# The first norm's sum of squares: eight products with ones on TensorE in place of seven adds on VectorE

## The chip, the cores and the metric

The kernel runs on one core of one Trainium2 chip. The metric is the device time of one execution in microseconds (us); a kernel's time is the median of its runs.

## The reference

One inference step of a two-layer decoder trunk over 576 tokens: 512 of a prompt and 8 sequences of 8 new tokens. The model is 1024 wide; everything is fp32.

```python
def rmsnorm(x, w):
    xf = x.astype(jnp.float32)
    y = xf * lax.rsqrt(jnp.mean(xf * xf, axis=-1, keepdims=True) + EPS)
    return (y * w.astype(jnp.float32)).astype(x.dtype)
...
def layer(x, ...):
    h = rmsnorm(x, P['norm_mix_w'][li])
    proj = jnp.einsum('bld,de->ble', h, P['w_in'][li]).astype(jnp.float32)
    (z, xbc, dt_raw, q_a, k_a, v_a, q_h, f_h, i_h, g_h, x_r, g_r) = jnp.split(proj, SPLIT_POINTS, axis=-1)
    # four mixers on the parts of proj: SSD (Mamba-2), sliding-window attention, HGRN2, RG-LRU
...
    mix = jnp.concatenate([y_ssd, y_swa, y_hg, y_lru], axis=-1).astype(dtype)
    x = x + jnp.einsum('ble,ed->bld', mix, P['w_out'][li])
    h2 = rmsnorm(x, P['norm_mlp_w'][li])
    up = jnp.einsum('bld,df->blf', h2, P['w_up'][li])
    x = x + jnp.einsum('blf,fd->bld', jnp.square(jax.nn.relu(up)), P['w_down'][li])
```

The norm that the change touches is the first `rmsnorm` of layer 0.

## The kernel before

x is held transposed: eight blocks `self.x[k]` of 128 features by 576 tokens. A product on TensorE has 128 features as its contraction and 288 tokens, half of them, as its columns; a weight matrix comes in tiles of 128 output columns with all 1024 features (`raw`, 512 KB each, loaded by SyncE's queue). To keep fp32 accuracy at the speed of the one-pass type fp32r, weights and activations are split into a high and a low part: `weight` (L326) makes `hi` on ScalarE and `lo` on VectorE, `norm` (L377, L378) makes `xh` on ScalarE and `xl` on VectorE, and each tile takes three products per feature block and half (`product`, L339): xh·hi, xl·hi, xh·lo, 24 to a half. The products of the projection are called `pi` in the profile.

The norm's weight is folded into `xh` and `xl`; the factor of each token, 1/sqrt(mean of squares + eps), is multiplied onto the finished products by VectorE (`put`, L419 to L423). So the products can run before the factor is known. `product` collects the first four finished halves in `self.waiting`, and with the fourth (`AHEAD` = 4) calls `rms`, in high priority. `rms` squares the eight blocks on ScalarE (L387, L391), adds them up in `ssq` on VectorE (L392) by way of `sq`, a tag with two buffers (`SQB`), and `rstd` multiplies ssq with a 128 by 128 matrix of ones on TensorE, one fp32 product a half (L402, into `ss`), which sums over the features and gives each partition the sum. ScalarE makes the factor of it by a logarithm (L403) and an exponential (L404). The first operations that need it are L423 for f, v and q, the first tiles of HGRN2.

Behind the first tiles, layer 0 goes on with HGRN2's first half, `hgrn(0)`: seven levels, each a chain on VectorE and ScalarE (t, c, kE, qE: L542 to L550) and then scores on TensorE (`sc`, L554), whose results VectorE copies into A under a mask (L562). Then come the HGRN norm (L623, L402 to L404), the step sizes of the SSD (`ssd_dt`: |b|, exponential, logarithm at L663 to L665, L666 on VectorE, transposes `dtt` on TensorE at L685, a transfer `acd` at L678 from which ScalarE's queue fetches the factors `cs`, `acj` and `a`), and the SSD itself, in two groups (`y` and `ys`, by `tiled`, L354). Weight products of the tiles to come stand between all these on TensorE.

No order is written out by hand: a scheduler places each instruction on its engine by priorities (`HP` = 3000 for what stands in `high_priority`) and by when its operands and buffers should be there. Each engine then works its list off in order, and waits at an instruction whose operands are not there. ScalarE needs a table for the functions it computes; a change of table is an instruction of its own, `ACT_TABLE_LOAD`.

Of the kernel before, what the change touches and what calls it, by code (L numbers as in the profile page):

```python
# [10 lines left out]
F32 = mybir.dt.float32  # L11
F32R = mybir.dt.float32r
U8 = mybir.dt.uint8
AF = mybir.ActivationFunctionType
ALU = mybir.AluOpType
# [8 lines left out]
T = NP_ + NS  # L24
TH = T // 2
DM = 1024
KD = DM // 128
# [12 lines left out]
SQB = 2  # L40
ORDER = (0, 4, 1, 5, 2, 6, 3, 7)
# [73 lines left out]
class Pool:  # L115


    def __init__(self, k, name, **kw):
        self.k = k
        self.cm = k.tc.tile_pool(name=name, bufs=1, **kw)  # L120
        self.pool = self.cm.__enter__()
# [27 lines left out]
class Kern:  # L149
    def __init__(self, ctx, tc, I, O):  # L150
        self.tc, self.nc, self.I, self.O = tc, tc.nc, I, O
        self.uid, self.nu, self.waiting, self.last = 0, 0, [], None
        P = lambda n, **k: ctx.enter_context(tc.tile_pool(name=n, bufs=1, **k))
        self.cp = P("const")
        self.wp = P("weights")
        self.np_ = P("normed")
        self.xp = P("x")
        self.lp = P("layer")
        self.tp = P("small")
        self.pm = P("pmm", space=PSUM)  # L160
        self.px = P("pmx", space=PSUM)
        self.dp = P("bounce", space=DRAM)
# [220 lines left out]
    def rms(self):  # L383
        nc = self.nc
        self.uid += 1
        acc = self.np_.tile([128, T], F32, name=f"ssq{self.uid}", tag="ssq")
        nc.scalar.activation(acc, self.x[0], AF.Square)  # L387
        for k in ORDER[1:]:
            self.uid += 1
            s = self.np_.tile([128, T], F32, name=f"sq{self.uid}", tag="sq", bufs=SQB)  # L390
            nc.scalar.activation(s, self.x[k], AF.Square)  # L391
            nc.vector.tensor_tensor(acc, acc, s, op=ALU.add)  # L392
        self.rstd(acc, [acc], 1.0 / DM, self.ones)
        return acc
# [1000 lines left out]
```

## Time and profile before

| | us |
|---|---|
| median of three runs | 1359.47 (1356.86 to 1362.58) |
| the profiled execution | 1355.2 |
| its span in the profile | 1353.4 |
| TensorE busy | 1328.0 (98%) |
| VectorE busy | 1028.5 (76%) |
| ScalarE busy | 658.2 (49%) |

PE is TensorE's products, PEld its weight loads, DVE VectorE, ACT ScalarE, POOL GpSimd. The rows of the section below are of five kinds. The busy line has an engine's busy time, its share of the span and, behind x, its instructions. A row of waits has engine, operation and line, what it waited for, and then us in all, times, and the longest. A row of windows has the stretch, its length, and the busy time (and instructions) of PE, PEld, DVE, ACT and POOL, then the granted clock of TensorE as a share of full speed, the DMA engines' share, and GB/s. A row of the chain has start, us, and what the end waited for in that time. A row of a timeline has start, busy us, engine, line, operation, out<-in, shapes, how many instructions it sums up, and in brackets the idle time before it and what ended it. Groups by line have busy us and mean ns of one.

### The profile page before, as it was taken

The numbers are of one execution on the slowest core, as the hardware profiler recorded it, in microseconds if no ns is written. First come the engines' busy times: TensorE is split into PE (matmuls) and PEld (weight loads), VectorE is DVE, ScalarE is ACT, GpSimd is POOL, SyncE is SP. The second block draws the span as 40 slices with busy tenths as digits, with TensorE's granted clock in tenths as the row PEclk, the third lists the DMA queues.
The fourth block names the chain that finished last, engine by engine and source line by source line (L and its number), as shares of the span: only waits on it lengthen the run. The fifth ranks groups of instructions, "written<-read, shape, count | busy, mean of one in ns | idle before, by whom it ended". The sixth has DMA issues, their size and how long they took to land.

```text
span 1353.4 us, 25452 instructions
## 1 busy us (share of the span) xinstructions
PE 1328.0 (98%) x10384; PEld 1279.6 (95%) x10384; DVE 1028.5 (76%) x2043; ACT 658.2 (49%) x1175; POOL 63.3 (5%) x126
## 2 busy tenths in 40 slices
PE   7999999999999999999999999999999999999997
PEld 7999899799999999999999998988999999999997
DVE  7788888488678677776669678886977677777755
ACT  6565436766243334333354774477653243334325
POOL 2201102000000000000000001100000000000000
PEclk9999999999999999999999999999999999999999
DMA  6324414123213222322331233231223213222312
GB/s 237 104 87 139 165 68 144 48 79 110 77 65 110 78 92 81 113 75 86 131 121 47 98 117 128 94 111 48 79 81 123 78 63 109 79 82 91 115 58 71
DMA packets 39831, 131.36 MB, mean 97 GB/s; under 512 B 6089, under 2 KB 8241, under 8 KB 39681
## 3 DMA queue, kind: packets, MB, share of 16 engines
q1 hardware_dynamic: 29312, 102.12, 21.9%
q0 software_dynamic: 6512, 22.64, 5.0%
q10 hardware_dynamic: 3888, 4.97, 1.2%
q8 instruction: 82, 1.34, 0.4%
q14 instruction: 37, 0.30, 0.1%
HBM read 120.32 MB, written 11.34 MB: 97 GB/s over the span
## 4 chain that ended last, share of the span: by engine, by line
PE 86%; DVE 7%; ACT 3%; issue 2%; DMA 0%; SPq 0%; DVEq 0%; ACTq 0%
PE pd L339 33%; PE p L1102 21%; PE pi L339 15%; PE pu L339 6%; PE pl L1255 2%; PE sc L554 2%; DVE lo L326 1%; DVE a L444 1%; PE ss L402 1%; PE ao L354 1%; ACT hi L326 1%; DVE A L562 1%; DVE qE L550 1%; PE y L354 1%; PE lg L978 1%
## 5 line engine op out<-in xcount | busy, mean ns | idle before, releaser
L326 ACT CAST hi<-raw 128x1024 fp32r<-128x1024 f32 x134 | 140.2, 1046 | 297.1 <-PE pd L339 144.6
L339 PE MATMUL pd<-fh,hi 128*128 128x288 f32 x960 | 284.1, 296 | 0.0
L339 PE MATMUL pd<-fl,hi 128*128 128x288 f32 x960 | 284.0, 296 | 0.0
L339 PE MATMUL pd<-fh,lo 128*128 128x288 f32 x960 | 282.8, 295 | 0.0
L339 PE MATMUL pi<-xh,hi 128*128 128x288 f32 x704 | 210.6, 300 | 7.6 <-ACT xh L377 7.1
L339 PE MATMUL pi<-xl,hi 128*128 128x288 f32 x704 | 210.4, 300 | 1.1 <-DVE xl L378 1.1
L339 PE MATMUL pi<-xh,lo 128*128 128x288 f32 x704 | 211.1, 300 | 0.0
L326 DVE TENSOR_TENSOR lo<-raw,hi 128x1024 fp32r<-128x1024 f32 x134 | 163.6, 1222 | 27.3 <-ACT hi L326 26.7
L1037 DVE TENSOR_TENSOR x<-x,pd 128x288 f32<-128x288 f32 x240 | 108.2, 451 | 97.9 <-PE pd L339 97.8
L339 PEld LDWEIGHTS pd<-fh,lo 128*128 128x128 f32 x960 | 180.9, 188 | 0.0
L339 PEld LDWEIGHTS pd<-fh,hi 128*128 128x128 f32 x960 | 180.4, 188 | 0.0
L339 PEld LDWEIGHTS pd<-fl,hi 128*128 128x128 f32 x960 | 180.4, 188 | 0.0
L339 PEld LDWEIGHTS pi<-xh,hi 128*128 128x128 f32 x704 | 133.0, 189 | 10.1 <-ACT xh L377 7.1
L339 PEld LDWEIGHTS pi<-xh,lo 128*128 128x128 f32 x704 | 132.9, 189 | 6.0 <-issue 5.2
L339 PEld LDWEIGHTS pi<-xl,hi 128*128 128x128 f32 x704 | 132.9, 189 | 3.6 <-DVE xl L378 1.7
L1102 PE MATMUL p<-Th,ul 128*128 128x288 f32 x312 | 92.2, 296 | 0.0
L1102 PE MATMUL p<-Tl,uh 128*128 128x288 f32 x312 | 92.1, 295 | 0.0
L1102 PE MATMUL p<-Th,uh 128*128 128x288 f32 x312 | 92.0, 295 | 0.0
L1102 PE MATMUL p<-xl,uh 128*128 128x288 f32 x312 | 91.9, 295 | 0.0
L1102 PE MATMUL p<-xh,ul 128*128 128x288 f32 x312 | 91.9, 295 | 0.0
L1102 PE MATMUL p<-xh,uh 128*128 128x288 f32 x312 | 91.7, 294 | 0.0
L1078 ACT CAST uh<-raw 128x1024 fp32r<-128x1024 f32 x52 | 54.5, 1048 | 66.8 <-PE p L1102 43.2
(489 smaller groups left out, 3003.2 us busy)
## 6 DMA issues: line engine op xcount, KB each, us to landing
raw<-in_wu SPq DMA_DIRECT2D x64, 512.0 KB, 3.3
raw<-in_wd SPq DMA_DIRECT2D x64, 512.0 KB, 4.2
raw<-in_wi SPq DMA_DIRECT2D x44, 512.0 KB, 3.3
raw<-in_wo SPq DMA_DIRECT2D x16, 512.0 KB, 3.2
x<-in_xT SPq DMA_DIRECT2D x8, 288.0 KB, 5.9
a<-acd ACTq DMA_DIRECT2D x4, 576.0 KB, 4.5
xl<-in_xT POOLq DMA_DIRECT2D x8, 288.0 KB, 4.3
xd<-x POOLq DMA_DIRECT2D x8, 288.0 KB, 2.4
```

Of the source, the lines that this page charges most:

```text
L326: self.split_ins = nc.scalar.copy(hi, raw).ins, nc.vector.tensor_tensor(lo, raw, hi.bitcast(F32), op=ALU.subtract).ins
L339: self.nc.tensor.matmul(out, w, x[:, a], start=n == 0, stop=n == last)
L354: self.nc.tensor.matmul(out, w, x, start=n < 2, stop=n >= len(products) - 2, skip_group_check=True)
L402: nc.tensor.matmul(ps[:, :TH], ones, s[:, TH * h : TH * h + TH], start=n == 0, stop=n == len(sqs) - 1)
L444: V.scalar_tensor_tensor(dst[:, :CW], src[:, k : k + CW], w(k), dst[:, :CW], op0=ALU.mult, op1=ALU.add)
L550: V.tensor_tensor(qE[r, d, : W // 2].rearrange("p (n h) -> p n h", h=h), qu[r], eu[r], op=ALU.mult)
L554: nc.tensor.matmul(pv[:, :, 64 * ci : 64 * ci + 64], kE[:, 128 * ci : 128 * ci + 128], qE[:, :, 64 * ci : 64 * ci + 64], start=True, stop= ...
L562: V.copy_predicated(Av[:, d], m, ps[:, d].rearrange("p (n h) -> p n h", h=h))
L1037: self.nc.vector.tensor_tensor(y[:, a], x[:, a], ps, op=ALU.add)
L1078: S.copy(hl[0], src)
L1102: nc.tensor.matmul(ps[:, :TH], u, x, start=j == 0, stop=j == 11)
L1255: nc.tensor.matmul(ps, u[:, o + q], v[:, a], start=j == 0, stop=j == 11)
```

## The change

For the first norm alone, eight squares are made in turn by ScalarE (the first, third, fifth, seventh) and VectorE, into the two `sq` buffers. Each square is multiplied with the ones on TensorE, one fp32 product a half, and the eight products of a half add up in one `ss` bank. There are no adds on VectorE. Logarithm and exponential are as before, and all other norms are unchanged.

```diff
-        self.uid, self.nu, self.waiting, self.last = 0, 0, [], None
+        self.uid, self.nu, self.waiting, self.last, self.first = 0, 0, [], None, True
...
         acc = self.np_.tile([128, T], F32, name=f"ssq{self.uid}", tag="ssq")
+        if self.first:
+
+            self.first = False
+            ss = [self.bank("ss")[:, :TH] for h in range(2)]
+            for n, k in enumerate(ORDER):
+                self.uid += 1
+                s = self.np_.tile([128, T], F32, name=f"sq{self.uid}", tag="sq", bufs=SQB)
+                if n % 2:
+                    nc.vector.tensor_tensor(s, self.x[k], self.x[k], op=ALU.mult)
+                else:
+                    nc.scalar.activation(s, self.x[k], AF.Square)
+                for h in range(2):
+                    nc.tensor.matmul(ss[h], self.ones, s[:, TH * h : TH * h + TH], start=n == 0, stop=n == KD - 1)
+            for h in range(2):
+                nc.scalar.activation(acc[:, TH * h : TH * h + TH], ss[h], AF.Ln, scale=1.0 / DM, bias=self.ceps)
+            nc.scalar.activation(acc, acc, AF.Exp, scale=-0.5)
+            return acc
         nc.scalar.activation(acc, self.x[0], AF.Square)
```

Lines from 404 on stand 17 further down in the changed kernel.

TensorE, right behind the first tile's two halves (pi_26, pi_27). Before, the second and third tile follow, with waits for their hi and lo, and the norm's two products come 26 products further on:

```order
L339 MATMUL pi_31_223<-xh11_119,hi30_219 128x288 [waits Activation_49]
L339 MATMUL pi_31_223<-xl11_120,hi30_219 128x288
L339 MATMUL pi_32_248<-xh11_119,hi30_219 128x288
L339 MATMUL pi_32_248<-xl11_120,hi30_219 128x288
L339 MATMUL pi_46_314<-xh11_119,hi45_310 128x288 [waits Activation_49]
L339 MATMUL pi_46_314<-xl11_120,hi45_310 128x288
L339 MATMUL pi_31_223<-xh11_119,lo30_220 128x288 [waits DVE_49]
...
L402 MATMUL ss_41_296<-ssq33_273,ones_110 128x288 [waits DVE_49]
L402 MATMUL ss_42_299<-ssq33_273,ones_110 128x288
```

In the changed kernel:

```order
L339 MATMUL pi_31_223<-xh11_119,hi30_219 128x288 [waits Activation_49]
L339 MATMUL pi_31_223<-xl11_120,hi30_219 128x288
L339 MATMUL pi_32_248<-xh11_119,hi30_219 128x288
L399 MATMUL ss_34_274<-sq36_276,ones_110 128x288
L399 MATMUL ss_35_275<-sq36_276,ones_110 128x288
...
L399 MATMUL ss_34_274<-sq38_284,ones_110 128x288 [waits Activation_49]
L399 MATMUL ss_35_275<-sq38_284,ones_110 128x288
L399 MATMUL ss_34_274<-sq39_288,ones_110 128x288 [waits DVE_49]
...
L399 MATMUL ss_35_275<-sq43_304,ones_110 128x288
L339 MATMUL pi_31_223<-xh11_119,lo30_220 128x288
```

The sixteen products with ones stand in one block, ahead of nearly all of the second tile; from the third square on each pair waits for the square, made in turn by ScalarE and VectorE.

The scheduler places the rest of layer 0's first stage anew as well, on all engines, up to the end of `hgrn(1)` (some 165 us in the profile before); behind that the order is the old one. The places on TensorE that come in between, with the weight products (pi) ahead of them since the start:

| ahead of | before | after |
|---|---|---|
| the scores of the fifth level (sc) | 430 | 407 |
| the HGRN norm's products (ss) | 515 | 475 |
| the first transpose dtt | 569 | 556 |
| y of the first SSD group | 689 | 704 |
| y of the second SSD group | 744 | 744 |
| between the last ys of the first group and y of the second | 55 | 31 |

VectorE ahead of the fifth level's qE, with a convolution of the SSD (L444, a), copies into A (L562) and the tile z (L423). Before:

```order
L444 SCALAR_TENSOR_TENSOR a_137_942<-X_136_941,prm_82,a_137_942 128x600 [waits DVE_49,Activation_49]
L444 SCALAR_TENSOR_TENSOR a_137_942<-X_136_941,prm_82,a_137_942 128x600 [waits DVE_49] x2
...
L562 COPY_PREDICATED A_19_157<-lmask_451,sc_76_538 128x64x4 [waits DVE_49] x2
L423 TENSOR_TENSOR z_146_1081<-pi_149_1088,ssq33_273 128x288 [waits PE_49]
L562 COPY_PREDICATED A_19_157<-lmask_451,scs_77_545 64x8x4 x2
L562 COPY_PREDICATED A_19_157<-lmask_451,sc_79_557 128x32x8 [waits DVE_49] x2
L546 TENSOR_TENSOR kE_20_158<-kk_60_464,t_80_564 128x16x16
L550 TENSOR_TENSOR qE_21_159<-q_43_307,t_80_564 64x256 x2
```

In the changed kernel:

```order
L579 COPY_PREDICATED A_19_157<-lmask_459,sc_77_546 128x64x4 [waits DVE_49] x2
L579 COPY_PREDICATED A_19_157<-lmask_459,scs_78_553 64x8x4 x2
L579 COPY_PREDICATED A_19_157<-lmask_459,sc_80_565 128x32x8 [waits DVE_49] x2
L436 TENSOR_TENSOR X_137_949<-pi_146_1050,ssq33_273 128x224 [waits PE_49]
L438 TENSOR_TENSOR X_137_949<-pi_146_1050,ssq33_273 128x8x8
L563 TENSOR_TENSOR kE_20_158<-kk_61_472,t_81_572 128x16x16
L326 TENSOR_TENSOR lo153_1151<-raw152_1148,hi153_1150 128x1024 [waits DMAHW3_49,Activation_49]
L567 TENSOR_TENSOR qE_21_159<-q_44_315,t_81_572 64x256 x2
```

One convolution step and the first half of z no longer stand ahead of qE.

ScalarE between the HGRN norm's logarithms and the acd transfer (b is the SSD's step size, X and z tiles that get a silu). Before:

```order
L403 ACTIVATE t_100_691<-ss_102_696,ceps_114 128x288 [waits PE_49]
L404 ACTIVATE t_100_691<-t_100_691 128x576 [waits Activation_49]
...
L459 CAST mixh_23_163<-o_66_485 128x576 [waits DVE_49]
L663 ACTIVATE b_104_707<-b_103_706 4x576
L504 ACTIVATE t_230_1694<-f_203_1432 128x576 [waits DVE_49]
L664 ACTIVATE b_104_707<-b_104_707 4x576 [waits Activation_49]
L505 ACTIVATE t_230_1694<-t_230_1694 128x576 [waits Activation_49]
L665 ACTIVATE b_104_707<-b_104_707,c1_112 4x576 [waits Activation_49]
...
L678 DMA acd0_731<-c_105_708 4x576 [waits DVE_49]
```

In the changed kernel (the logarithms have a load ahead of them too, and four more follow L682 ahead of the transfer):

```order
L421 ACT_TABLE_LOAD
L421 ACTIVATE t_101_699<-t_101_699 128x576 [waits Activation_49]
L680 ACTIVATE b_105_715<-b_104_714 4x576 [waits DVE_49]
L357 ACT_TABLE_LOAD
L357 ACTIVATE X_137_949<-a_138_950 128x2x512
...
L681 ACT_TABLE_LOAD
L681 ACTIVATE b_105_715<-b_105_715 4x576 [waits Activation_49]
...
L682 ACT_TABLE_LOAD
L682 ACTIVATE b_105_715<-b_105_715,c1_112 4x576 [waits Activation_49]
L357 ACT_TABLE_LOAD
```

The silu of X and z, ahead of the HGRN norm before, now stand among the operations of b, with a change of table at each turn. In the whole program there are 39 table loads for 35.

## Rows read from the trace of the kernel before

**Rows 1.** The page's busy line, and the chain that ended last by engine.

```profile
PE 1328.0 (98%) x10384; PEld 1279.6 (95%) x10384; DVE 1028.5 (76%) x2043; ACT 658.2 (49%) x1175; POOL 63.3 (5%) x126
...
PE 86%; DVE 7%; ACT 3%; issue 2%; DMA 0%; SPq 0%; DVEq 0%; ACTq 0%
```

**Rows 2.** TensorE's waits, 0 to 200 us.

```profile
PE pi L339 <- ACT xh L377: 7.1, 1, 7.1
PE y L354 <- issue: 1.5, 1, 1.5
```

**Rows 3.** Windows of two stages.

```profile
50.00:97.00 47.00, 46.87 (x413) 45.91 (x413) 39.20 (x85) 27.08 (x40) 1.01 (x3) 1.00 0.20 69
97.00:150.00 53.00, 51.48 (x417) 44.41 (x415) 42.92 (x89) 25.87 (x41) 8.51 (x18) 1.00 0.44 146
```

**Rows 4.** The chain that ended last, 17 to 50 us.

```profile
22.95 8.51 PE pi L339 x64
```

**Rows 5.** Groups by line, 5 to 24 us.

```profile
L392 DVE TENSOR_TENSOR ssq<-ssq,sq 128x576 f32<-128x576 f32 x7 | 5.3, 754 | 0.1
L391 ACT ACTIVATE sq<-x 128x576 f32<-128x576 f32 x7 | 4.7, 677 | 1.7 <-DVE lb L307 1.1 <-DVE ssq L392 0.5
```

**Rows 6.** Timelines of VectorE and ScalarE around the norm.

```profile
31.48 0.46 DVE L423 TENSOR_TENSOR q<-pi,ssq 128x288 f32<-128x288 f32 x1 [1.55 <-PE pi L339]
...
16.80 1.03 ACT L326 CAST hi<-raw 128x1024 fp32r<-128x1024 f32 x1
...
22.50 0.99 ACT L403 ACTIVATE ssq<-ss,ceps 128x288 f32<-128x288 f32 x2 [1.74 <-PE ss L402]
```

**Rows 7.** TensorE's timeline at the norm's two products.

```profile
21.63 0.30 PE L339 MATMUL pi<-xh,lo 128*128 128x288 f32 x1
21.76 1.19 PE L402 MATMUL ss<-ssq,ones 128*128 128x288 f32 x4
...
22.91 0.29 PE L339 MATMUL pi<-xl,hi 128*128 128x288 f32 x1
```

**Rows 8.** TensorE's timeline at the second tile's beginning.

```profile
17.06 0.29 PE L339 MATMUL pi<-xl,hi 128*128 128x288 f32 x1
17.88 0.40 PE L339 MATMUL pi<-xh,hi 128*128 128x288 f32 x1 [0.53 <-ACT hi L326]
...
18.46 0.29 PE L339 MATMUL pi<-xh,hi 128*128 128x288 f32 x1
```

**Rows 9.** VectorE's and TensorE's timelines at the fifth level.

```profile
78.41 0.84 DVE L550 TENSOR_TENSOR qE<-q,t 64x256 f32<-64x256 f32 x2
79.28 0.84 DVE L444 SCALAR_TENSOR_TENSOR a<-X,prm,a 128x600 f32<-128x600 f32 x1
...
79.35 1.11 PE L554 MATMUL sc<-qE,kE 128*128 128x128 f32 x8
```

**Rows 10.** Timelines of ScalarE, VectorE and TensorE, 89 to 112 us.

```profile
89.07 1.28 ACT L357 ACT_TABLE_LOAD   x1
90.36 1.17 ACT L357 ACTIVATE z<-z 128x1152 f32<-128x1152 f32 x1
...
99.55 0.99 ACT L403 ACTIVATE t<-ss,ceps 128x288 f32<-128x288 f32 x2 [1.36 <-PE ss L402]
...
106.73 0.76 ACT L665 ACTIVATE b<-b,c 4x576 f32<-4x576 f32 x1
...
111.33 0.51 ACTq L678 DMA_DIRECT2D acd<-c  x1
...
107.52 0.74 DVE L666 SCALAR_TENSOR_TENSOR b<-b,b 4x576 f32<-4x576 f32 x1 [0.88 <-ACT b L665]
...
108.41 0.19 PE L685 MATMUL dtt<-cst,b 4*128 4x4 f32 x1
```

**Rows 11.** Timelines of ScalarE and TensorE ahead of the second group's y.

```profile
143.82 1.05 ACT L326 CAST hi<-raw 128x1024 fp32r<-128x1024 f32 x1 [1.99 <-PE pi L339]
...
148.61 1.09 PE L354 MATMUL y<-a,c 128*64 128x128 f32 x16 [1.52 <-issue]
```

## Prediction

> **What bounds the kernel now.** I read the busy line first [rows 1]: TensorE works 1328.0 us, 98% of the span, and the chain that ended last is TensorE for 86%. The reader is to see that an instruction added to TensorE has almost nowhere to hide. How much is that "almost"? TensorE's waits of the first 200 us [rows 2] begin with 7.1 us for the first block of x, which the change leaves alone; behind the start the longest is 1.5 us. By stage [rows 3] TensorE is busy 46.87 of 47.00 us from 50 to 97 us and 51.48 of 53.00 from 97 to 150, while VectorE has 8 and 10 us free there and ScalarE 20 and 27. The granted clock is 1.00. Last comes the chain where the changed norm stands [rows 4]: behind the norm's own products, from 22.95 us, it runs through 64 weight products on TensorE, and only then to VectorE. So the norm's arithmetic on ScalarE and VectorE is not what the end waits for; TensorE is.
>
> **The change part by part.**
>
> *Off ScalarE and VectorE.* Seven adds of 754 ns go, and of eight squares at 677 ns four move to VectorE [rows 5]. A square on VectorE is not in the trace; the nearest row is the add with the same shape, so I take 0.75 us, with 0.68, ScalarE's price, as the other end. VectorE has three operations less, −2.3 us, and ScalarE four squares less, −2.7. Who waits for that? VectorE idles 1.55 us ahead of q, the HGRN chain's first operation, for TensorE's weight products [rows 6]. As long as q waits for them, the relief is worth nothing. Without that cover it could be worth up to 2.3.
>
> *Onto TensorE.* Two ones-products become sixteen. Their price: the weight product ahead of the two starts at 21.63, the first of the two at 21.76, the second weight product behind them at 22.91 [rows 7]. So a weight product takes 0.13 us, and the pair 22.91 − 21.63 − 2 × 0.13 = 1.02, which is 0.51 for one fp32 product. Fourteen more: **+7.1 us**.
>
> *A stall that goes.* At 17.06 TensorE stops for the second tile's high half, resumes at 17.88 and then steps unevenly to 18.46 [rows 8]; that is 1.40 us for four products worth 0.52. The block of sixteen starts where this stall was and runs 8.2 us, by which time both halves are there: **−0.9 us**. Behind the block TensorE is 6.2 us late.
>
> *Do the sixteen wait for their squares?* There are two buffers: the third square overwrites the first, once the first's pair of products has ended. A turn is a pair, the handover to the other engine, the square, and the handover back. From the norm's products to ScalarE it takes 22.50 − 21.76 − 0.51 = 0.23 [rows 6, 7], from ScalarE to TensorE 17.88 − 16.80 − 1.03 = 0.05 [rows 6, 8]. So 1.02 + 0.23 + 0.68 + 0.05 = 1.98 us on ScalarE and 2.05 on VectorE, against the 2.04 that two pairs take. It just closes. I take 0, and keep as the other bound a square for which TensorE waits in full, six times 0.75 = 4.5 us.
>
> *What is late next.* The new order gives TensorE fewer weight products ahead of what it waits for later (the table in the section on the change), while ScalarE and VectorE start their chains 6.2 us late with no less to do in them. I follow three places, in times of the profile, the common 6.2 us left out.
>
> (1) The fifth level's scores, 79.35. The last operand qE ends at 78.41 + 0.84 = 79.25: a margin of 0.1 us [rows 9]. With 23 weight products less ahead TensorE comes 23 × 0.13 = 3.0 us earlier, at 76.3. VectorE has one convolution step (0.84) and one z (like q, 0.46) less ahead [rows 6, 9], so qE ends near 77.9: **+1.6 us**, 0.3 if VectorE finds another 1.3 in its idle time.
>
> (2) dtt, 108.41. Its operand b ends on VectorE at 107.52 + 0.74 = 108.26, a margin of 0.15 [rows 10]. With 13 products less ahead TensorE is there at 106.7, with the wait at (1) 108.3. ScalarE's way from the HGRN norm's logarithms (99.55) to the end of L665 (106.73 + 0.76 = 107.49) took 7.9 us. In the new order it holds the logarithms 0.99, two casts hi of 1.05 [rows 11], four operations 576 wide like the squares (0.68), a silu like z's 1.17, four table loads of 1.28, and L665's 0.76: 12.9 us. It starts 40 × 0.13 = 5.2 us earlier, less the wait at (1) and one table load ahead of it, so 2.3 earlier. L665 ends near 110.1, b near 110.9, and TensorE waits about **+2.6 us**; 0 if the chain's start is as much earlier as TensorE's place alone would allow.
>
> (3) y of the second group, 148.61, where TensorE already waits 1.52 us [rows 11]. Behind L665 ScalarE has four more table loads, z, a short silu (0.3 by my estimate from z's) and the exponential of c before the acd transfer that y's factors come from: 110.1 + 5.1 + 1.2 + 0.3 + 0.7 = 117.4, where it was issued at 111.33 [rows 10]. That is 6.1 us late; TensorE is 4.2 late by (1) and (2), but from the first group's last product to y it has 24 weight products (3.1 us) less. On ScalarE 1.99 us of idle time at a cast [rows 11] can give way. Between 6.1 and 4.1 I take 5.0 in all, **+0.8 us** here.
>
> Table loads deserve a look, as the program has four more. In the trace a load takes 1.28 us and the next instruction starts 0.01 later: 89.07 + 1.28 = 90.35, z at 90.36 [rows 10]. The Trainium skill, "ScalarE: Activation LUTs", section "What ACT_TABLE_LOAD costs", gives about 1283 ns for the load and adds about 1380 ns for a drain at each change of set. The first figure is the trace's; the second does not show between these rows, so the measurement decides. By the page the four loads would bring 4 × 1.38 = 5.5 us more, an estimate from its figure.
>
> **Sum.** 7.1 − 0.9 + 1.6 + 2.6 + 0.8 = 11.2 us; I take 0.7 off, since a later TensorE shortens some of its small waits for other engines behind this stage: **+10.5 us**. The profiled execution took 1355.2 us, 4.3 less than the median of three runs, 1359.47 (1356.86 to 1362.58). So 1365.7 for an execution like it, and **1370.0** against the median.
>
> **The rivals.**
>
> *A, only the products count.* The three later waits don't come, since ScalarE and VectorE have free time in each stage [rows 3] and start relieved. +6.2, so 1365.7 us. Against it: margins of 0.1 and 0.15 us at (1) and (2), with less cover at both. 0.26.
>
> *B, not slower.* The products of the block are cheaper than the pair in the trace, because sixteen in a row share their stationary operand, the ones. At half the price, 0.26 us, it is 14 × 0.26 − 0.9 = +2.7 and 1362.2 us; at a weight product's 0.13 it is +0.9 and 1360.4. With the later waits, 4.3 us after what I took off, added it decides below 0.24 us a product, where the whole is under 6.8 us, 0.5%. Against it: the pair at 21.76 shares its ones as well and took 0.51 each [rows 7]. 0.08. A real gain would need over 6.2 us of TensorE's waits to go, and behind the start the longest is 1.5 [rows 2].
>
> *C, the block waits for its squares.* From one handover 0.4 us later in each turn of two blocks (3 × 0.4 = 1.2) to the full 4.5: 1371 to 1374.5 us. For it: the turn closes with nothing to spare. 0.10.
>
> *D, a change of table empties ScalarE first.* Each of four extra loads then costs about another load's time on the way to dtt and y, 4 × 1.28 = 5.1: 1375.1 us. Against it: the gap of 0.01 us [rows 10]. 0.04. This is the mechanism of the Trainium skill's section named above.
>
> **How the numbers follow.** My forecast, the products and the later waits at between a quarter and one and a half times their price (+7.5 to +13, so 1367 to 1372.5), has 0.50; A 0.26, B 0.08, C 0.10, D 0.04; 0.02 is left for a gain that I don't see. The range goes from B's dearer end to D: 1361.5 to 1375. Half a per cent, 6.8 us, is about what these runs can tell from no change: the border is 1366.3. A lies at it, mostly below (0.18 of its 0.26), B below (0.07), of the forecast 0.05: same 0.30, faster 0.03, slower 0.67.
>
> **What would show it.** In the changed profile: sixteen L399 products that take 8 us from about 17 us on, TensorE's busy time up by about 7, no wait for hi near 17.9, and q on VectorE about 6 us later, still waiting for TensorE. Then waits of TensorE that the kernel before has not: over 1 us for qE in the fifth level, over 2 for b at dtt, over 2 in all at y. If the block is there and the waits are missing, A is right. Waits for "sq" inside the block are C. I am wrong if the block takes under 5 us, or if the difference appears behind 165 us, where the order is the old one.

## The result, and the profile after

The changed kernel takes 1375.15 us (median of 6 runs, 1371.73 to 1378.81), the kernel before beside it 1356.88 (6 runs, 1355.73 to 1362.58): a ratio of 1.0128, 95% interval 1.0103 to 1.0154, or +18.3 us where +10.5 was forecast. The profiled execution took 1371.73 us, with a span of 1369.9, 16.5 more than before.

The page's busy line of the changed kernel:

```profile
PE 1342.0 (98%) x10412; PEld 1290.2 (94%) x10412; DVE 1027.9 (75%) x2040; ACT 661.0 (48%) x1175; POOL 62.5 (5%) x126
```

TensorE is busy 14.0 us longer with 28 more records, two for each of the fourteen new products [rows 1]. At 0.51 us these cost 7.1. So half of the added busy time is something else. Its waits from 0 to 200 us (us in all, times, longest), beside [rows 2]:

```profile
PE pi L339 <- ACT xh L377: 7.2, 1, 7.2
PE dtt L702 <- DVE b L683: 2.3, 1, 2.3
PE y L354 <- issue: 1.9, 1, 1.9
...
PE sc L571 <- DVE qE L567: 0.5, 1, 0.5
```

The wait for b at dtt is new, that at y has grown from 1.5 to 1.9, and the 0.5 for qE belong to an earlier level and were there before. In TensorE's timeline, the block, and dtt with what follows (a bracket is the idle time before):

```profile
17.31 0.30 PE L339 MATMUL pi<-xh,hi 128*128 128x288 f32 x1
17.45 8.37 PE L399 MATMUL ss<-sq,ones 128*128 128x288 f32 x32
...
25.79 0.29 PE L339 MATMUL pi<-xh,hi 128*128 128x288 f32 x1
...
115.93 0.19 PE L702 MATMUL dtt<-cst,b 4*128 4x4 f32 x1 [2.35 <-DVE b L683]
116.06 1.12 PE L258 MATMUL rb<-x,rb 32*128 32x128 f32 x8
...
118.37 1.36 PE L753 MATMUL G<-X 64*128 64x128 f32 x6
...
120.31 0.44 PE L339 MATMUL pi<-xh,hi 128*128 128x288 f32 x1
120.55 0.44 PE L339 MATMUL pi<-xl,hi 128*128 128x288 f32 x1
...
164.15 1.09 PE L354 MATMUL y<-a,c 128*64 128x128 f32 x16 [1.92 <-issue]
```

Behind the wait, and behind small fp32 products (dtt, rb, tr, G), a weight product starts every 0.24 us and not every 0.13. The windows say why (length, busy PE, PEld, DVE, ACT, POOL, then the granted clock):

```profile
20.00:113.00 93.00, 92.32 (x725) 84.53 (x724) 66.73 (x138) 48.34 (x78) 8.48 (x17) 1.00 0.26 87
113.00:118.00 5.00, 2.65 (x20) 2.13 (x19) 4.11 (x6) 4.94 (x6) 0.00 (x0) 1.00 0.33 105
118.00:132.00 14.00, 14.00 (x66) 12.64 (x66) 4.66 (x11) 6.24 (x9) 2.56 (x6) 0.53 0.19 69
132.00:165.00 33.00, 31.08 (x268) 27.78 (x267) 26.42 (x57) 16.24 (x23) 3.47 (x8) 0.99 0.50 155
```

From 118 to 132 us the granted clock is 0.53: TensorE runs at 1.2 and not 2.4 GHz for 2 × 0.47 × 14 = 13.2 us and loses 6.6. PE is "busy" for 14.00 of 14.00 us there, which is why the busy line grew.

The stage in steps, by rows of equal place in both kernels. Behind the block, the first product that makes `dtq`, the step sizes' part of the projection, comes 6.7 us late; the first row is from before, the second from the changed kernel:

```profile
37.73 2.15 PE L644 MATMUL dtq<-x,w 128*32 128x288 f32 x32
44.43 2.15 PE L661 MATMUL dtq<-x,w 128*32 128x288 f32 x32
```

dtt comes at 115.93 for 108.41 with 13 weight products less ahead of it (1.7 us): 9.2 late. y of the second group, with as many products ahead as before, at 164.15 for 148.61 [rows 11]: 15.5. The end of the span: 16.5.

Each run gives its span and mean granted clock. Clock times span is the length that the run would have at full clock if TensorE's work filled it ("at full clock" below); the rest is put down as lost to half clock. Some 3 us of each "lost" cost nothing: in the profile of before the clock falls behind TensorE's last product (0.68 from 1345 to 1350 us, 0.50 from there to the end), so what counts is the difference to before. Clocks are given to a thousandth, so a value is good to some 0.7 us; medians over the runs, 16 to 21 runs of before beside the experiments. One of e10's eleven runs, a slow one of 2162.09 us at a clock of 0.556, is left out.

| kernel | median us | ratio to before, 95% interval | at full clock | lost |
|---|---|---|---|---|
| before | 1356.9 to 1357.3 | | 1352.3 | 3 |
| changed | 1375.15 | 1.0128 (1.0103 to 1.0154) | 1359.6 | 13 |
| e1 fp32 block, old order | 1362.31 | 1.0048 (1.0031 to 1.0066) | 1357.5 | 3 |
| e2 one-pass block, new order | 1376.52 | 1.0139 (1.0120 to 1.0159) | 1356.8 | 18 |
| e3 one-pass block, old order | 1357.40 | 0.9993 (0.9981 to 1.0005) | 1353.0 | 3 |
| e4 fp32 block, new order, no wait at dtt | 1368.90 | 1.0083 (1.0068 to 1.0097) | 1357.5 | 10 |
| e5 before, one load on b's path | 1360.72 | 1.0030 (1.0016 to 1.0044) | 1353.5 | 5 |
| e6 before, two loads on b's path | 1365.80 | 1.0056 (1.0040 to 1.0072) | 1354.2 | 10 |
| e7 squares in turn, adds kept | 1371.07 | 1.0088 (1.0065 to 1.0110) | 1351.6 | 18 |
| e8 sixteen products, own order | 1371.09 | 1.0094 (1.0071 to 1.0116) | 1361.0 | 8 |
| e9 before, b first | 1357.42 | 1.0006 (0.9997 to 1.0015) | 1351.2 | 5 |
| e10 one-pass block, b first | 1357.96 | 1.0008 (0.9994 to 1.0022) | 1352.1 | 4 |

So of the changed kernel's 18 us some 7 are work and waits at full clock, and some 10 are half clock. In the profiled execution it is 16.5 − 6.6 = 9.9 and 6.6.

### The profile page after: what moved, and what is told of

It reads as the page before. It is cut to its first block, busy times and chain, and to the rows that moved or that the text cites. A ratio compares the mean times of both kernels' runs of the same rounds, so it can differ in the third digit from the quotient of the medians.

```text
span 1369.9 us, 25506 instructions
## 1 busy us (share of the span) xinstructions
PE 1342.0 (98%) x10412; PEld 1290.2 (94%) x10412; DVE 1027.9 (75%) x2040; ACT 661.0 (48%) x1175; POOL 62.5 (5%) x126
## 4 chain that ended last, share of the span: by engine, by line
PE 89%; DVE 4%; ACT 4%; issue 2%; DMA 1%; DVEq 0%; ACTq 0%
PE pd L339 32%; PE p L1119 21%; PE pi L339 18%; PE pu L339 6%; PE sc L571 2%; PE pl L1272 2%; DVE lo L326 1%; PE ss L419 1%; PE ao L354 1%; PE ss L399 1%; ACT hi L326 1%; PE lg L995 1%; PE pt L1019 1%; PE o L354 1%; DVE xl L1054 0%
```

## The experiments

The theory after the result: the block costs what it was priced at; the new order makes TensorE wait at dtt; and behind that wait, in a stretch of small products, its clock falls. The first rival (theory 2) has the fall come from the fp32 products themselves. A second (theory 3, taken up with e5 and e6) has it come from the new order as a whole and not from a wait.

**Order and price apart (e1, e2, e3).** The scheduler knows how long a product takes, so a change of type changes its order too. With squares and ones in the one-pass type fp32r it returns to the order of before behind the block (569 weight products ahead of dtt and 35 table loads, as before). That is e3:

```diff
+        self.onesr = cp.tile([128, 128], F32R, name="onesr")
+        nc.vector.tensor_copy(self.onesr, self.ones)
...
-                s = self.np_.tile([128, T], F32, name=f"sq{self.uid}", tag="sq", bufs=SQB)
+                s = self.np_.tile([128, T], F32R, name=f"sq{self.uid}", tag="sq", bufs=SQB)
...
-                    nc.tensor.matmul(ss[h], self.ones, s[:, TH * h : TH * h + TH], start=n == 0, stop=n == KD - 1)
+                    nc.tensor.matmul(ss[h], self.onesr, s[:, TH * h : TH * h + TH], start=n == 0, stop=n == KD - 1)
```

For e1 and e2 the operands' type was exchanged once the order was set: e1 is e3's order with fp32 products, e2 the changed kernel's order with one-pass products.

```diff
+    for fn in nc.m.functions:
+        for bb in fn.blocks:
+            L = list(bb.instructions)
+            for j, i in enumerate(L):
+                if i.name in names:
+                    L[j] = i.__replace__(ins=tuple(x.__replace__(dtype=F32) for x in i.ins))
```

> Sixteen fp32 products with ones in the block, but the rest of the stage in the order of before (35 table loads, as before). Theory 1 (block, then a wait at dtt, then a fall of TensorE's clock behind that wait): the block alone, +6.2 to +7 us over before, no wait over 0.5 us at dtt, and no stretch of half clock between 20 and 300 us. Theory 2 (the clock falls because of the fp32 products or of a heavier TensorE, and the wait only happens to be near): a fall here as well, +13 to +17 us.

Measured: +5.0 us by the medians (+4 to +9 by the interval). TensorE's waits from 20 to 200 us and a window of its profile:

```profile
PE y L356 <- issue: 1.5, 1, 1.5
```

```profile
110.00:130.00 20.00, 20.00 (x152) 18.14 (x151) 14.83 (x31) 9.37 (x16) 2.57 (x6) 1.00 0.39 124
```

No wait at dtt, clock 1.00 where the changed kernel has 0.53. Sixteen fp32 products alone bring down no clock in this profile; theory 2 falls, and e2 and e7, with a fall and without those products, speak against it too. Three of e1's eight runs are 5 to 7 us longer than the other five, at a mean clock of 0.994; four of the nineteen runs of before beside it are at 0.994 or 0.995 as well. Where the clock falls in such runs no profile shows.

> The order of the changed kernel word for word, but the sixteen products in the one-pass type (squares and ones as fp32r), so that the block takes 2.1 us and not 8.2. Theory 1: 6.1 us less than the changed kernel, no more; the wait at dtt stays at 2 to 2.5 us, since ScalarE's chain moves with the block, and the clock falls behind it: +10 to +13 us over before. Theory 2: no fall without the fp32 products: +1 to +4 us.

Measured: +19 us, the changed kernel's time without its expensive products. The fall that theory 1 asked for is there, the number is missed by 6 to 9 us. Waits from 10 to 200 us, and two windows:

```profile
PE dtt L704 <- DVE b L685: 2.3, 1, 2.3
PE y L356 <- issue: 2.2, 1, 2.2
PE ss L401 <- DVE sq L397: 2.0, 3, 0.8
PE ss L401 <- ACT sq L399: 0.7, 1, 0.7
```

```profile
110.00:130.00 20.00, 17.65 (x103) 15.71 (x102) 9.02 (x17) 12.20 (x16) 2.57 (x6) 0.74 0.22 74
...
160.00:178.00 18.00, 17.03 (x98) 12.94 (x99) 11.40 (x29) 6.68 (x18) 3.44 (x6) 0.53 0.27 87
```

Two things eat the saving. One-pass products are through before the next square is, and the block waits 2.7 us for its squares, which the fp32 products hid. And the clock falls a second time, behind the wait of 2.2 us at y. At full clock e2 is 2.8 us below the changed kernel, at half clock it loses 5 more.

> Sixteen one-pass products (squares and ones as fp32r), scheduled as such, which gives the order of before behind the block. Both theories: 16 x 0.13 - 1.02 for the block and -0.9 for the stall, +0.2 us over before within 1.5, no wait at dtt, no fall of the clock.

Measured: as before, within the interval of −2.6 to +0.7 us. Its code differs from the changed kernel's in that type alone, and with the order that follows from it all of the 18 us are gone.

**The wait at dtt taken away (e4).** In the changed kernel's order, every silu of layer 0 is computed as a copy once the order is set; X and z so keep their raw values.

```diff
-        return self.nc.scalar.activation(out, in_, AF.Silu)
+        i = self.nc.scalar.activation(out, in_, AF.Silu)
+        if self.li == 0:
+            self.named.add(i.ins.name)
+        return i
...
+                L[j] = L[j].__replace__(func=AF.Copy)
```

> The changed kernel with its order and its fp32 block, but layer 0's silu computed as a copy (X and z keep their raw values), so that the table loads around the silu of X fall away and b is ready when TensorE comes to dtt. Theory 1: without the wait no fall: +6.5 to +8.5 us over before. Theory 2: the fall stays, and only the 2.3 us of the wait go: +14 to +17.

Measured: +11.6 us, between the two. ScalarE's timeline on b's way, first the changed kernel's with VectorE's last step, then e4's:

```profile
101.42 0.89 ACT L420 ACTIVATE t<-ss,ceps 128x288 f32<-128x288 f32 x2
...
104.50 1.28 ACT L421 ACT_TABLE_LOAD   x1
...
107.07 1.28 ACT L357 ACT_TABLE_LOAD   x1
108.36 1.06 ACT L357 ACTIVATE X<-a 128x1024 f32<-128x1024 f32 x1
...
110.00 1.28 ACT L681 ACT_TABLE_LOAD   x1
...
112.94 1.28 ACT L682 ACT_TABLE_LOAD   x1
114.23 0.77 ACT L682 ACTIVATE b<-b,c 4x576 f32<-4x576 f32 x1
...
115.04 0.75 DVE L683 SCALAR_TENSOR_TENSOR b<-b,b 4x576 f32<-4x576 f32 x1 [0.86 <-ACT b L682]
```

```profile
102.06 0.99 ACT L423 ACTIVATE t<-ss,ceps 128x288 f32<-128x288 f32 x2 [1.06 <-PE ss L422]
...
111.64 0.78 ACT L685 ACTIVATE b<-b,c 4x576 f32<-4x576 f32 x1
```

Four loads, 5.1 us, stand between the logarithms and b; without them b is ready and the wait at dtt is gone. So is the fall behind it, and another stands at the next place. Windows of e4, and its longest wait from 100 to 200 us:

```profile
110.00:130.00 20.00, 20.00 (x146) 17.44 (x146) 12.26 (x25) 8.92 (x13) 2.91 (x8) 1.00 0.35 119
...
157.00:178.00 21.00, 21.00 (x138) 16.97 (x134) 14.31 (x36) 8.18 (x21) 6.19 (x11) 0.67 0.32 105
```

```profile
PE y L354 <- issue: 1.9, 1, 1.9
```

In five runs of five e4 lost 8 to 11 us to half clock. So the fall at dtt belongs to the wait at dtt, as theory 1 has it. But theory 1 knew only one place. The fall at y cost 6.9 us (0.33 × 21), more than the 3 to 5 by which its number failed.

**Waits alone, in the kernel before (e5, e6).** The order and the norm are those of before; once the order was set, functions on b's way were exchanged for others of the table of silu, so that b takes other values: in e5 the logarithm at L665, in e6 |b| by a silu and two exponentials by squares.

```diff
-        S.activation(t1, t1, AF.Ln, bias=self.c1[:4])
+        i = S.activation(t1, t1, AF.Ln, bias=self.c1[:4]).ins
+        if self.li == 0:
+            self.named[i.name] = AF.Silu
```

> The kernel before in its own order, its norm untouched, with one table load put on b's path: the logarithm at L665 is computed as a silu (b is wrong by that), which costs a load of 1.28 us, and two more loads behind it. b had a margin of 0.15 us, so TensorE waits about 1.1 us at dtt. Theory 1 (a wait of TensorE in this stretch of small products brings the clock down, whatever made the wait): +1.1 us, and if 1.1 us are already enough for a fall, 3 to 8 us on top; the kernel before had 1.5 us of wait at y without a fall, so I expect none: +1 to +2.5. Theory 3 (the new order as a whole, not a wait, brings the clock down): +1.1 and no fall.

> As the one before, with two loads on b's path (|b| computed as a silu, the exponentials of b and of the second HGRN half as squares): TensorE waits 2.57 - 0.15 = 2.4 us at dtt, as in the changed kernel, in the order of before and without one additional product. Theory 1: the clock falls behind that wait as in the changed kernel, +2.4 for the wait and 5 to 10 for the fall, +7 to +13 us over before. Theory 3: +2.4 to +3.5, clock at 1.00 throughout.

Measured: +3.5 us for e5 and +8.6 for e6 by the medians. e6's timeline of TensorE and its window:

```profile
112.80 0.19 PE L691 MATMUL dtt<-cst,b 4*128 4x4 f32 x1 [2.83 <-DVE b L672]
...
117.63 0.45 PE L339 MATMUL pi<-xh,hi 128*128 128x288 f32 x1
117.87 0.45 PE L339 MATMUL pi<-xl,hi 128*128 128x288 f32 x1
```

```profile
110.00:130.00 20.00, 17.20 (x108) 15.17 (x109) 11.17 (x24) 7.92 (x12) 2.58 (x6) 0.83 0.29 95
```

A wait of 2.8 us, made by table loads in an otherwise untouched order, brings the clock down behind it; theory 3 falls. At full clock e6 is only 1.9 us over before, 7 more are half clock, and each of its six runs lost 5 us or more (3 in the median of before). e5, with waits of 1.4 and 0.75 us at two transposes dtt, fell too, against my expectation:

```profile
110.00:130.00 20.00, 18.93 (x101) 16.63 (x102) 10.39 (x23) 6.85 (x11) 2.58 (x6) 0.66 0.33 99
```

**Other ways to the same place (e7, e8).** e7 makes the squares in turn and keeps the adds; e8 keeps squares and adds and multiplies the finished sum eight times (`self.rstd(acc, [acc] * 8, 1.0 / (8 * DM), self.ones)` for the first norm). Both are scheduled on their own. e7's edit:

```diff
+            if first and n % 2 == 0:
+                nc.vector.tensor_tensor(s, self.x[k], self.x[k], op=ALU.mult)
+            else:
+                nc.scalar.activation(s, self.x[k], AF.Square)
```

> Squares in turn on ScalarE and VectorE as in the change, but added up on VectorE as before, two products with ones in all. It is scheduled on its own, in an order that has much of the changed kernel's (38 table loads, 31 weight products between the first group's ys and y of the second). If the new order is what costs, this kernel pays for it without the block: a wait at dtt or y of over 1.5 us and a fall of the clock, +5 to +12 us. If the products are what costs, it is within 2 us of before.

> Squares and adds as before, and the finished sum multiplied with the ones eight times over (scaled by an eighth): sixteen fp32 products as in the change, nothing taken from ScalarE and VectorE, scheduled on its own (37 table loads, dtt 36 weight products later than before). The block alone costs +7.1; the stall that the change removed stays. Theory 1: +7 to +8 if b is ready at dtt (36 weight products more ahead make it so) and y waits less than 1.6 us; with a wait of 2 us at y and a fall, +14 to +18.

Measured: +13.9 us each by the medians, for e7 more than the +5 to +12 of its expectation, for e8 a little under its +14 to +18. e7 has no product more than the kernel before and is no longer at full clock (0.7 us less, which is as good as such a value is); its cost is all half clock. Its waits from 100 to 200 us and windows:

```profile
PE y L354 <- issue: 2.1, 1, 2.1
PE dtt L689 <- DVE b L670: 1.5, 1, 1.5
```

```profile
110.00:130.00 20.00, 18.52 (x87) 16.25 (x85) 11.15 (x22) 6.09 (x12) 2.60 (x6) 0.57 0.27 93
...
157.00:178.00 21.00, 19.12 (x123) 15.18 (x124) 13.84 (x35) 6.93 (x18) 5.39 (x10) 0.67 0.30 97
```

e8 pays for the products (+8.7 at full clock), has no wait over 0.2 us at dtt, and falls behind waits of 1.4 and 2.2 us at the two y (granted clock 0.87 from 130 to 157 us and 0.59 from 157 to 178).

**Can it be had without?** (e9, e10) b's chain, |b| to L666, in high priority for layer 0, on the kernel before and on e3:

```diff
+        with self.tc.high_priority(HP if self.li == 0 else 0):
+            S.activation(t1, dt, AF.Abs)
```

> The kernel before with b's chain (|b| to L666) of layer 0 in high priority. The scheduler then puts dtt 5 and y of the first group 14 weight products earlier, and leaves 69 and not 55 weight products between the two groups (35 table loads as before). If waits in these two places and what follows from them is what moves the time, the wait of 1.5 us at y of the second group goes (14 x 0.13 = 1.8 us more cover), at the risk of a new one at y of the first: -1 to -3 us against before, and fewer of the runs that lie 3 to 6 us higher. If only TensorE's work counts: 0 within 1.

> The squares in turn and sixteen one-pass products, and b's chain in high priority on top: behind the block the order of the kernel with b first (dtt at 564, y at 675 and 744 weight products). The block is worth 0 to +1 against before as in the kernel with the cheap block in the old order, the later order the same as with b first: -2 to +1 us against before.

Measured: no change for either, e9 −0.4 to +2.0 us and e10 −0.8 to +3.0 by their intervals; the −1 to −3 expected of e9 did not come. In e9 the wait at y of the second group shrinks to 1.1 us, and a new one of 0.4 stands at y of the first. At full clock e9 is a microsecond shorter than before; half clock takes that back. e10's longest wait from 100 to 200 us is 0.5 us, and yet its clock falls twice in its profile:

```profile
110.00:130.00 20.00, 19.89 (x135) 17.48 (x133) 13.90 (x32) 5.92 (x11) 3.29 (x8) 0.91 0.43 142
...
157.00:178.00 21.00, 21.00 (x133) 18.77 (x132) 16.79 (x44) 8.68 (x22) 3.57 (x7) 0.87 0.45 151
```

No version ran that beats the kernel before; e3 is its equal.

## Why the prediction was right, and where it fell short

*TensorE bounds the stage; the norm on the other engines doesn't count*: right. e3 takes the same squares and adds off ScalarE and VectorE as the change does, with products at a quarter of the price, and gains nothing (ratio 0.9993, 0.9981 to 1.0005). In the changed kernel VectorE still idled ahead of q for TensorE's weight products, 2.74 us at 38.18, where it was 1.55 at 31.48.

*Fourteen products, +7.1*: right. The sixteen take 25.79 − 17.31 − 2 × 0.13 = 8.2 us, 0.51 each. Rival B, cheaper products with the ones kept in place, falls with it.

*The stall, −0.9, and no wait for squares*: right; TensorE was 6.7 us late behind the block where 6.2 was forecast, 0.1 of it from x, for which it waited 7.2 us and not 7.1; the other 0.4 were not traced. No wait inside the block, so rival C falls, but e2 shows how near it was: with cheaper products 2.7 us of waits appear.

*(1) The fifth level, +1.6*: wrong. The changed kernel's rows on VectorE and TensorE:

```profile
82.32 0.85 DVE L567 TENSOR_TENSOR qE<-q,t 64x256 f32<-64x256 f32 x2
...
82.93 0.29 PE L339 MATMUL pi<-xl,hi 128*128 128x288 f32 x1
83.22 0.49 PE L571 MATMUL sc<-qE,kE 128*128 128x128 f32 x2
```

A product started at 82.93 and took its 0.13, and the scores came 0.16 later. VectorE had been tied to TensorE at q and found the rest of the time in its idle stretches, which is the lower bound given there (0.3).

*(2) dtt, +2.6*: right in its place, its cause and its size, 2.35 us. L682 ends 114.23 + 0.77 − 101.42 = 13.6 us after the logarithms began; 12.9 was forecast. e4 shows that the loads are the cause. Table loads cost what the rows before showed, 1.28 us with the next instruction 0.01 to 0.02 behind them (107.07 + 1.28, X at 108.36), so rival D falls. By the Trainium skill, "ScalarE: Activation LUTs", section "What ACT_TABLE_LOAD costs", 1.38 us more would have come on top of each; no row here shows it.

*(3) y, +0.8*: 0.4 in the profile, 1.9 for 1.5, and not by the way that was forecast. The sum put ScalarE's loads, z and the exponential of c ahead of the acd transfer and had it 6.1 us late on top of the common 6.2. ScalarE's timeline of the changed kernel:

```profile
118.92 0.52 ACTq L695 DMA_DIRECT2D acd<-c  x1
119.17 1.16 ACT L357 ACTIVATE z<-z 128x1152 f32<-128x1152 f32 x1
...
121.65 0.68 ACT L693 ACTIVATE c<-c 4x576 f32<-4x576 f32 x1
```

The transfer was issued before z and the exponential ran, 7.6 us later than before in all (118.92 for 111.33), and 45 us ahead of y. The last step ahead of y is VectorE's on its operand a, from 162.82 to 164.24.

*What was missing from the sum*: a term for TensorE's clock. The prediction read a granted clock of 1.00 [rows 3] and priced each wait at its own length. In the changed kernel the wait at dtt cost 2.35 us and the half clock behind it 6.6 in the profiled execution; the median run lost some 10 more than before, in places that no profile shows. That is the miss: +18.3 us measured for +10.5 forecast, 7.8 too little. It looks like 5 (1375 for 1370) only because the forecast was counted from a median of 1359.47, and the kernel before took 1356.88 beside the changed one. What the sum did contain came to 9.9 us in the profiled execution and to 7.3 by the medians, though (1) did not come and (3) came another way. The profile of before could have raised the question: dtt, with its margin of 0.15 us, and y, with its wait of 1.5, both stand where TensorE does small products in place of weight products.

*The range*: 1375.15 lies at its upper end, 1375, which was set by rival D. As D's mechanism did not appear, it is luck that the range reaches so far; of the forecast itself, 1367 to 1372.5, the median lies outside.

*Rival A, only the products*: not this kernel, but e1 is rival A made real: +5.0 us by the medians for +6.2 forecast, with an interval that holds both (+4.2 to +9.0).

What stays open is what a fall costs. It isn't proportional to the wait: e5, with 1.4 and 0.75 us, had a granted clock of 0.66 from 110 to 130 us in its profile, e6, with 2.8, had 0.83, and the changed kernel's runs lie between 0.987 and 0.993 in their means. Nor does every wait bring one: behind the 1.9 us at y the changed kernel's clock stayed up in its profile, and e4's fell behind 1.9 us at the same place. Nor does it need a wait of that length: e10 shows two falls with none over 0.5 us, and in e3 the clock is 0.91 from 110 to 130 us, and TensorE doesn't wait there at all.

```profile
110.00:130.00 20.00, 20.00 (x132) 17.09 (x132) 14.54 (x32) 6.42 (x14) 3.65 (x9) 0.91 0.41 129
```

What differs between two runs of one kernel was not tried.

## What to carry to other kernels

A change that adds work to the bounding engine is read in two parts: its price, which rows of the same instruction give, and what the scheduler does with the price. Here the price was 5 to 7 us and the new order 11 to 13, and e2 paid for the order, 19 us, without the work; the two do not simply add up. Where a schedule is made from costs, compare the orders first, and look for table loads on a path that had a margin of 0.15 us. And a wait on TensorE in a stretch of small products is priced with the half clock that may follow it, not at its own length.

## What the runs showed of the hardware that was not expected

TensorE's clock fell to 1.2 GHz at or behind waits of 1.4 to 2.8 us that stand among small fp32 products (at dtt in the changed kernel, e2, e5, e6 and e7; at y in e2, e4, e7 and e8), and stayed at 1.00 behind the wait of 1.5 us at y in the profiles of before, e1, e3, e5 and e6 and behind the 1.9 us at y in the changed kernel's. e3 and e10 fell without such a wait (0.91 from 110 to 130 us in both, 0.87 from 157 to 178 in e10). What TensorE did before all these falls was transposes and other small products in place of weight products, in all but e3's and e10's with a wait of 1.4 us or more. The Trainium skill, "TensorE: Matmul & The Clock Gate", section "HAM oscillation — how this bites in real kernels", tells of a kernel whose waits between short bursts of products take the clock down again and again. The traces agree where a wait went before the fall, and the loss (6.6 us in the changed kernel's profile) is larger here than the wait; e3's fall, without one, is not of that kind.

The spread among the changed kernel's runs is the clock: its six runs span 7 us, from 1371.73 at a mean clock of 0.993 to 1378.81 at 0.987, and clock times span is 1358.4 to 1361.0 in all six.
